# A two-layer encoder on one core: memory and x transposed raw, the norm's weights in the splits, the rows' factor behind the products

## The chip, the cores and the metric

The kernel runs on one core of one Trainium2 chip. The metric is the device time of one execution in microseconds, from the first instruction to the end. The engines are PE (matrix products and transposes), DVE (VectorE), ACT (ScalarE), POOL (GpSimd) and SP, which only issues transfers; ACT and POOL issue some too.

## The reference

Two layers over 512 tokens of width 1024 and 256 memory tokens. All data are float32.

```python
def rmsnorm(x, g):
    y = x * lax.rsqrt(jnp.mean(x * x, axis=-1, keepdims=True) + EPS)
    return y * g

for i in range(2):
    h = rmsnorm(x, norm_g[i])
    mem_h = rmsnorm(mem, mem_norm_g[i])
    proj = h @ w_in[i]                      # mixer heads, memory queries, gate
    o_mix = mixer_dilated(...) if i == 0 else mixer_axial_gqa(...)
    o_mem = memory_attention(q_mem, mem_h, w_mem_kv[i], ...)
    y = concatenate([o_mix, o_mem]) * silu(gate)
    x = x + y @ w_out[i]
```

In both mixers, and in memory attention, each head's queries and keys go through an rmsnorm of their own (128 wide, with the same EPS) before the scores. Layer 0 has 8 heads with three groups of queries, keys and values each; group 0 looks at nearby tokens, groups 1 and 2 at tokens of the same residue mod 4. Layer 1 has 8 query heads on 2 key and value heads.

What matters for the change: a row's norm is a factor r per token times a weight g per feature. A projection of h is r times a projection of g * x, since r belongs to the row and comes out of the sum over features. A head's rmsnorm of r * p with EPS equals the rmsnorm of p with EPS / r**2.

## The kernel before

**Products.** A float32 product is made of three passes over operands split in two: `mm3` multiplies high by high, high by low and low by high, where the high part is the operand rounded to the matrix format and the low part is the remainder. A split is a copy on ACT into the rounded type and a subtraction on DVE (`split`, L156).

**Weights.** `Weights` (L182) streams all weights as pieces of 128x1024, 512 KB each, over SP's queue. `dma` (L229) loads while fewer than `KEEP[...]` pieces are live; `hi` (L278) makes the high part on ACT (L287), `lo` (L292) the remainder on DVE (L297), in a ring of 4. Kinds `T2` and `T2b` are the key and value weights of memory in the layers 0 and 1, eight pieces each. All other projections are products of 2 x 2 blocks with seven block products in place of eight, for which weight pieces are also summed, by DVE (L256) or by adding transfers that POOL issues (`sum`, L243).

**Order.** All engines' instructions are put in order by hand, by one `Driver`. A slot is one step of the weight stream: some 12 products of 128x512 or 24 of 128x256 on PE, then `W.advance()` (splits of weights to come) and `drv.tick()`, which runs every generator that is due: `spawn(gen, delay)` sets one up `delay` slots ahead, `yield n` puts its next step n slots later. `late` and `soon` put a call behind or ahead of a slot's steps.

**Blocks of x.** `s_chunk` (L356) is a projection of x. Its seven products need, in this order, the parts "12", "11", "S1", "S2", "S4", "S3" and "22" of the transposed activation H: blocks of 256 tokens by 512 features and sums or differences of them, each in a high and a low part. Where a part isn't set up yet, the loop ticks on without a product. `evac` results go to `ev` functions that norm, rotate and store.

**The start.** Memory is loaded as two tiles of 128x1024, x as four; the two norm weight rows come as single rows. Eight products with a row of ones (`row_bank`, L585) spread the weight rows over all partitions in PSUM. `norm_1` (L454) makes a row's factor: squares on ACT (one on DVE), and sum, EPS and power -0.5 on POOL (`rstd_of`, L419). `norm_2` (L467) multiplies by the factor and the weights on DVE. `turn4` (L471) transposes four 128x128 blocks on PE, and splits them. Then `mem_kv` (L621) projects memory to keys and values in eight slots; `ahead` (L950), called between its products, norms and transposes the rest of memory. `prep` (L893), spawned in slot `PD`, norms x and makes the parts of H, 128 tokens at a time, with `first_t`, `diffs_t` and `rest_t`. Keys are normed and transposed right after their projection (`ev_k`), values are split (`ev_v`).

**After the start.** The first `s_chunk` is the value projection of group 0, stored to memory as `v0d` and loaded back head by head (`load_v0`, L1104). Then come the memory queries, eight head chunks (`head_chunk`, L1012), each followed by its attention (`attn_a`, L1056) spread over later slots, and three gate chunks m, a and b (`gate`, L749), which apply the gate to attention results loaded from memory. `out_proj` closes the layer; meanwhile `mem_norm(1)` (L595) loads, norms and transposes memory again with the weights of layer 1, and `ev_o` (L1232) norms the new x for the second layer, which goes on in the same way.

## Time and profile before

| | |
|---|---|
| three runs | 967.74, 972.62, 973.62 us; median 972.62 |
| span of the profiled execution | 967.0 us |
| mean granted TensorE clock | 1.000 |
| power steps of row factors and head norms on POOL (L424) | 98, 1059 ns each |
| weight remainders on DVE (L297) | 255, 1237 ns each |
| high parts of weights on ACT (L287) | 255, 1059 ns each |

How to read the profile: times are microseconds unless marked ns. A row of a group has line, engine, operation, written and read tiles, shapes and count, then busy time, mean ns of one, and the idle time of the engine just before with what ended it. A row in time order has start, duration, engine, line, operation, tiles and count, and in brackets the idle time before it. A row of waits has who waited for whom, the total, the number and the longest. A row of stages has the stretch, its length, busy time and count for PE, PEld (weight load), DVE, ACT and POOL, the granted clock, the busy share of the transfer engines and GB/s. L12 is line 12 of the kernel. Matmuls are pipelined and their ends are modelled: the pace of PE is read from start to start.

### The profile page before, as it was taken

How to read it: one execution, taken by the hardware profiler on the slowest of the kernel's cores; microseconds unless marked ns; L12 is line 12 of the kernel's file. 1: busy time of each engine (PE TensorE's matmuls, PEld its weight loads, DVE VectorE, ACT ScalarE, POOL GpSimd, SP SyncE). 2: the span in 40 equal slices, each digit the busy share in tenths (PEclk: the TensorE clock that was granted, in tenths of full speed). 3: DMA queues.
4: the chain of work that ended last, by engine and by line, in shares of the span. 5: the costliest groups of instructions: out<-in, count | busy, mean ns of one | idle time of the engine just before them, and what ended most of it. 6: DMA issues, size and time to landing. Idle time of an engine off the chain costs nothing.

```text
span 967.0 us, 16588 instructions
## 1 busy us (share of the span) xinstructions
PE 946.3 (98%) x5682; PEld 831.4 (86%) x5682; DVE 789.8 (82%) x1411; ACT 682.8 (71%) x1701; POOL 344.3 (36%) x482
## 2 busy tenths in 40 slices
PE   8999999999999999999999999999899999999998
PEld 5879888888888888888899996788899999998786
DVE  5898676888888888888888899779878897769773
ACT  5775689686768686868685657447778887878770
POOL 1513423556554545454726011234333330011011
PEclk9999999999999999999999999999999999999999
DMA  9989956969686868785959889879776686877744
GB/s 357 318 228 344 266 115 170 293 122 268 153 254 141 263 148 257 156 258 132 283 132 252 245 189 305 285 212 362 202 175 137 189 233 168 225 200 177 202 131 131
DMA packets 89129, 209.81 MB, mean 217 GB/s; under 512 B 25298, under 2 KB 36050, under 8 KB 89044
## 3 DMA queue, kind: packets, MB, share of 16 engines
q1 hardware_dynamic: 69892, 145.76, 43.8%
q0 software_dynamic: 17856, 60.83, 33.3%
q10 hardware_dynamic: 1296, 2.16, 0.6%
q8 instruction: 45, 0.74, 0.3%
q14 instruction: 40, 0.33, 0.1%
HBM read 157.27 MB, written 12.65 MB: 176 GB/s over the span
## 4 chain that ended last, share of the span: by engine, by line
PE 80%; DVE 8%; DMA 7%; ACT 3%; issue 1%; SPq 0%; DVEq 0%; ACTq 0%
PE pj L164 21%; PE pj L166 21%; PE pj L165 20%; DVE wo L297 2%; DMA og<-od 2%; PE qT L569 2%; PE ptb L1386 1%; PE sa L1087 1%; PE oo L1189 1%; DMA od<-o 1%; DMA v<-v0d 1%; DMA wl<-in_wall_dram 1%; PE sa L1083 1%; PE pt L1168 1%; PE ob L165 1%
## 5 line engine op out<-in xcount | busy, mean ns | idle before, releaser
L297 DVE TENSOR_TENSOR wo<-wl,wh 128x1024 fp32r<-128x1024 f32 x255 | 314.0, 1237 | 6.2 <-ACT wh L287 6.0
L287 ACT CAST wh<-wl 128x1024 fp32r<-128x1024 f32 x255 | 268.9, 1059 | 53.4 <-PE pj L166 35.5
L164 PE MATMUL pj<-wh,hS 128*128 128x512 f32 (+1 forms) x448 | 163.8, 366 | 0.7 <-ACT sn L364 0.7
L165 PE MATMUL pj<-wo,hS 128*128 128x512 f32 (+1 forms) x448 | 158.2, 353 | 4.3 <-DVE wo L297 4.3
L166 PE MATMUL pj<-wh,hS 128*128 128x512 f32 (+1 forms) x448 | 158.3, 353 | 0.0
L164 PE MATMUL pj<-wh,h 128*128 128x512 f32 (+1 forms) x336 | 122.5, 365 | 0.0
L165 PE MATMUL pj<-wo,h 128*128 128x512 f32 (+1 forms) x336 | 118.5, 353 | 0.1
L166 PE MATMUL pj<-wh,h 128*128 128x512 f32 (+1 forms) x336 | 118.6, 353 | 0.0
L424 POOL TENSOR_TENSOR rstd<-mse,half 128x4 f32<-128x4 f32 (+2 forms) x98 | 103.8, 1059 | 8.2
L165 PEld LDWEIGHTS pj<-wo,hS 128*128 128x128 f32 x448 | 85.0, 190 | 15.4 <-DVE wo L297 5.3
L166 PEld LDWEIGHTS pj<-wh,hS 128*128 128x128 f32 x448 | 84.8, 189 | 12.1
L164 PEld LDWEIGHTS pj<-wh,hS 128*128 128x128 f32 x448 | 84.9, 189 | 11.3 <-ACT sn L364 1.3
L423 POOL TENSOR_SCALAR mse<-hss 128x4 f32<-128x4 f32 (+1 forms) x86 | 46.5, 541 | 126.6 <-ACT junk L557 122.8
L364 ACT COPY sn<-pj 128x512 f32<-128x512 f32 x132 | 73.7, 590 | 19.2 <-PE pj L166 17.9
L557 ACT ACTIVATE junk<-sn 128x128 f32<-128x128 f32 x264 | 79.0, 307 | 1.9 <-DVE sn L375 1.9
L1031 POOL TENSOR_TENSOR ta<-sn,tabs 128x128 f32<-128x128 f32 (+1 forms) x64 | 37.3, 583 | 119.7 <-DVE sn L562 91.5
L381 DVE TENSOR_TENSOR sn<-pj,sn 128x512 f32<-128x512 f32 x99 | 67.6, 685 | 5.6 <-PE pj L166 5.1
L166 PEld LDWEIGHTS pj<-wh,h 128*128 128x128 f32 x336 | 63.6, 189 | 8.9
L165 PEld LDWEIGHTS pj<-wo,h 128*128 128x128 f32 x336 | 63.8, 190 | 8.1 <-DVE wo L297 0.8
L164 PEld LDWEIGHTS pj<-wh,h 128*128 128x128 f32 x336 | 63.7, 190 | 7.2
L271 POOL DMA_DIRECT2D wl<-wl x33 | 29.1, 882 | 113.8 <-DVE wo L297 59.6
L164 PE MATMUL pj<-hS,wh 128*128 128x256 f32 x192 | 56.0, 292 | 0.0
(231 smaller groups left out, 2466.0 us busy)
## 6 DMA issues: line engine op xcount, KB each, us to landing
wl<-in_wall_dram SPq DMA_DIRECT2D x222, 512.0 KB, 6.9
wl<-wl POOLq DMA_DIRECT2D x66, 512.0 KB, 5.9
wl<-in_wall_dram POOLq DMA_DIRECT2D x42, 512.0 KB, 8.6
acc<-sn POOLq DMA_DIRECT2D x16, 256.0 KB, 4.5
od<-o SPq DMA_DIRECT2D x12, 256.0 KB, 5.6
og<-od SPq DMA_DIRECT2D x12, 256.0 KB, 6.1
odb<-o SPq DMA_DIRECT2D x12, 256.0 KB, 3.3
og<-odb SPq DMA_DIRECT2D x12, 256.0 KB, 4.5
```

Of the source, the lines that this page charges most:

```text
L164: T.matmul(o, lh, rh, start=start, stop=False, skip_group_check=True)
L165: T.matmul(o, lh, rl, start=False, stop=False, skip_group_check=True)
L166: T.matmul(o, ll, rh, start=False, stop=stop, skip_group_check=True)
L271: G.dma_start(self.tile[key], self.tile[c, "T2", x], accum_op=ALU.add)
L287: A.copy(wh, self.tile[self.items[i]])
L297: V.tensor_tensor(wo, self.tile[key], wh.bitcast(F32), ALU.subtract)
L364: A.copy(t, b)
L381: V.tensor_tensor(t, b, t, ALU.subtract if q == "12" else ALU.add)
L423: G.tensor_scalar(e, ss, EPS, None, ALU.add)
L424: G.tensor_tensor(r, e, half[:, 0:n], ALU.pow)
L557: A.activation(jk, p[:, j * 128:(j + 1) * 128], AF.Square, scale=QS, accum_out=ss[:, j:j + 1])
L1031: G.tensor_tensor(ta[:, 0:n], xn[:, 0:n, 0:32], ropeA[:, 0, b, s0:s0 + n], ALU.mult)
```

## The change

- Memory and x are no longer normed before they are transposed. The raw rows are transposed. The norm's weights, loaded as 32 rows of 128 and transposed once into a column per block (`gain`), are multiplied in where the operand is split: for x in `gain_hi` (ACT) and `gain_lo` (DVE) and in the sums (`gain_add`), for memory in the split of the key and value weights (`gain_of`, in `hi` and `lo`).
- `prep` makes each part of H for all 256 tokens at once, in its own order; one difference (for "S3") is made on POOL.
- The rows' factors come later: `Rows.square` and `Rows.finish` for memory (`mem_rows`, spawned in slot 9) and x (`x_rows`, slot 11). Keys and values that are projected before memory's factor is there are copied raw to SBUF, and normed or scaled later (`raw`, `kv_raw`).
- Behind the products: head norms get EPS times (mean square + EPS) in place of EPS (`head_sq(..., eps)`); values of groups 1 and 2 are scaled as they are copied; group 0's values are scaled in `scale_v0` on POOL, once a head; gates are multiplied by the factor per token, `rb`, spread over partitions, on POOL (chunks m and a) or DVE (chunk b), with one more slot between. x's factors go through memory to change their layout.
- For layer 1 memory is loaded raw again and only transposed; x of layer 1 is normed as before.
- The row products are gone; two products of a constant tile (512 and 128 columns) stand at the start. Memory, x and the first weight piece are loaded in halves. In the first part of the key projection both token blocks use the first weight piece before the second.
- `chunk` takes all its PSUM banks at its start; constants: `PD` 2 to 3, `KEEP_1` 9 (was 10) for the first blocked chunk.

```diff
         def hi(self, force=False):
...
-            A.copy(wh, self.tile[self.items[i]])
+            g = self.gain_of(i)
+            if g is None:
+                A.copy(wh, self.tile[self.items[i]])
+            else:
+                for k in range(2):
+                    cs = slice(k * 512, (k + 1) * 512)
+                    A.activation(wh[:, cs], self.tile[self.items[i]][:, cs], AF.Copy, scale=g[:, k:k + 1])
...
-            V.tensor_tensor(wo, self.tile[key], wh.bitcast(F32), ALU.subtract)
+            g = self.gain_of(i)
...
+                    V.scalar_tensor_tensor(wo[:, cs], self.tile[key][:, cs], g[:, k:k + 1], wh[:, cs].bitcast(F32), ALU.mult, ALU.subtract)
...
+    def gain_hi(hi, src, g, ks=range(4)):
+        for k in ks:
+            A.activation(hi[:, k], src[:, k], AF.Copy, scale=g[:, k:k + 1])
+
+    def gain_lo(lo, src, g, hi, ks=range(4)):
+        for k in ks:
+            V.scalar_tensor_tensor(lo[:, k], src[:, k], g[:, k:k + 1], hi[:, k].bitcast(F32), ALU.mult, ALU.subtract)
+
+    def gain_add(dst, src, g, other):
+        for k in range(4):
+            V.scalar_tensor_tensor(dst[:, k], src[:, k], g[:, k:k + 1], other[:, k], ALU.mult, ALU.add)
...
     def prep():
...
+        turned(0)
+        yield 1
+        turned(1)
+        yield 1
+        yield from scaled("12", xr[0, 1], gx[1])
+        turned(2)
+        yield 1
+        yield from scaled("11", xr[0, 0], gx[0])
+        turned(3)
+        yield 1
+        u = m4(name="xu").rearrange("p (k t) -> p k t", k=4)
+        for k in range(4):
+            A.activation(u[:, k], xr[1, 1][:, k], AF.Copy, scale=gneg[:, 4 + k:5 + k])
+        yield 1
+        gain_add(u, xr[1, 0], gx[0], u)
+        G.tensor_tensor(xr[1, 0], xr[0, 0], xr[1, 0], ALU.subtract)
+        yield 1
+        yield from plain("S1", u)
+        yield 1
+        gain_add(xr[0, 0], xr[0, 0], gneg[:, 0:4], u)
+        yield 1
+        yield from plain("S2", xr[0, 0])
+        yield 1
+        gain_add(xr[0, 1], xr[0, 1], gx[1], xr[0, 0])
+        yield 1
+        yield from plain("S4", xr[0, 1])
+        yield 1
+        yield from scaled("S3", xr[1, 0], gx[0])
+        yield 1
+        yield from scaled("22", xr[1, 1], gx[1])
...
+    mem_tiles()
+    mem_load(0, 0)
+    W.dma(1, True)
+    mem_load(1, 0)
+    W.dma(1)
+    mem_load(0, 1)
+    mem_load(1, 1)
+    W.dma(2)
+    for c in range(4):
+        x_load(c)
         W.dma(1)
...
+    for n in (512, 128):
+        T.matmul(at("idle")[:, 0:n], idle[:, 0:128], idle[:, 0:n], start=True, stop=True)
...
+    mem_turn(M, mem_nat, 0, 0)
     W.hi(True)
+    W.lo()
+    mem_turn(M, mem_nat, 1, 0)
     W.hi(True)
     W.lo()
...
+        def scale_v0():
+            G.tensor_tensor(v0, v0, r0s[:, :, None].to_broadcast([128, 4, 128]), ALU.mult)
...
         scale(1)
         yield Y[6]
+        scale_v0()
         scale(0)
         turn(1)
...
+                if rb is not None:
+                    tv = t.rearrange("p (h t) -> p h t", h=2)
+                    (V if g == 2 else G).tensor_tensor(tv, tv, rb[:, None, ts].to_broadcast([128, 2, 256]), ALU.mult)
+                    yield 1
                 th = s2(name="th")
                 A.activation(th, t, AF.Tanh, scale=0.5)
```

`scaled(k, ...)` is `gain_hi`, one slot, `gain_lo`, and the part is set up; `plain(k, ...)` the same with a plain copy and subtraction. `turned(c)` transposes 128 tokens of x and copies them to SBUF on ACT.

More of the change, by code (lines that the diff above doesn't have):

```diff
@@ L331, in trunk_kernel, with chunk @@
     W = Weights()
-    def chunk(units, nb, group, evac, pre=None):
-        ps = [None] * nb
+    def chunk(units, nb, group, evac):
+        ps = [pj() for _ in range(nb)]
         for u in range(units):
@@ L551, in rest_t, with head_sq @@
         yield 1
-    def head_sq(p, n=4):
+    def head_sq(p, n=4, eps=None):
         ss = sm(n, "hss")
@@ L881, in trunk_kernel @@
         W.dma(1)
-    W.dma(2)
-    tabA = s2(name="tabA")[:, 0:256].rearrange("p (b c d) -> p b c d", b=2, c=4)
-    grA = s2(name="grA")[:, 0:192].rearrange("p (s c) -> p s c", s=6)
     nc.sync.dma_start(gc, gcol)
-    for c in range(4):
-        nc.sync.dma_start(xt[c], xv[c])
-        if c % 2:
-            W.dma(2)
     H, H2 = {}, {}
-    xb = [halves(t) for t in xt]
-    def prep():
-        n = {}
-        for c in range(5):
-            if c < 4:
-                n[c] = norm_1(xb[c])
-            if c:
-                norm_2(xb[c - 1], n[c - 1], rows["x"])
-            if 1 < c < 4:
-                first_t(H, xb[c - 2], c - 2)
-            yield 1
-        for c in range(2):
-            yield from diffs_t(H, xb[2 + c], c)
-            drv.spawn(rest_t(H, c, (2, 2, 2)), 1)
-            yield 1
+    gx = [gain[:, 4 * j:4 * j + 4] for j in range(2)]
@@ L972, in ev_v0 @@
         yield 1
-    km, vm = mem_kv(0, M, ahead)
+    km, vm = mem_kv(0, M, between)
     s_chunk(512, H, ev_v0)
@@ L990, in ev_qm @@
         i, j = int(q[0]) - 1, int(q[1]) - 1
-        r = head_sq(t)
+        r = head_sq(t, 4, RX.eps[:, 2 * i:2 * i + 2])
         yield 1
```

276 lines of the change are left out of this document (175 added, 101 removed).

## The prediction

> **What bounds the kernel now.** I read the page first, then the busy time of each engine by stage, then who kept PE waiting, and last the first microseconds in order of time, because most of the edit lies there. From the page:
>
> ```profile
> span 967.0 us, 16588 instructions
> ...
> PE 946.3 (98%) x5682; PEld 831.4 (86%) x5682; DVE 789.8 (82%) x1411; ACT 682.8 (71%) x1701; POOL 344.3 (36%) x482
> ```
>
> PE is busy nearly all the time, and the edit takes no product away: what can be won is time in which PE stands still, in all 967.0 - 946.3 = 20.7 us, plus time that it spends on work that is not a product. Busy time by stage (PE, PEld, DVE, ACT, POOL):
>
> ```profile
> 0.00:30.00 30.00, 26.74 (x90) 17.47 (x91) 15.84 (x22) 19.49 (x43) 8.42 (x19) 1.00 0.94 369
> 30.00:80.00 50.00, 48.42 (x225) 38.86 (x224) 48.74 (x61) 34.89 (x60) 17.16 (x18) 1.00 0.91 257
> ...
> 200.00:500.00 300.00, 300.00 (x1578) 254.59 (x1577) 251.93 (x572) 219.51 (x660) 161.48 (x242) 1.00 0.75 199
> 500.00:545.00 45.00, 45.00 (x377) 44.89 (x376) 37.10 (x81) 27.54 (x71) 18.29 (x27) 1.00 0.87 244
> 560.00:600.00 40.00, 38.16 (x222) 32.34 (x221) 39.15 (x67) 26.52 (x40) 6.07 (x7) 1.00 1.00 252
> 600.00:640.00 40.00, 37.59 (x187) 30.94 (x186) 29.77 (x40) 20.47 (x34) 9.07 (x12) 1.00 0.86 267
> ```
>
> The reader is to see two stretches in which DVE, not PE, has no room: 30 to 80 us (48.74 of 50) and 560 to 600 us (39.15 of 40). In the head stage, 200 to 500 us, DVE has 48 us of room and PE none. PE's own waits, first for 0 to 100 us, then for 560 to 700 us:
>
> ```profile
> PE pj L165 <- DVE wo L297: 1.5, 2, 0.9
> PE pj L164 <- ACT act L158: 0.9, 2, 0.7
> ```
>
> ```profile
> PE pj L165 <- DVE wo L297: 4.2, 3, 2.9
> ```
>
> **The change part by part.** First the start, which stands in time order:
>
> ```profile
> 0.73 0.35 SPq L874 DMA_DIRECT2D row<-in_mem_norm_g_dram  x1
> 1.42 0.37 SPq L880 DMA_DIRECT2D m<-in_mem_dram  x1
> 1.83 0.43 SPq L238 DMA_DIRECT2D wl<-in_wall_dram  x1
> 2.35 7.16 PE L590 MATMUL row<-row,tabs 1*128 1x512 f32 x8 [2.35 <-DMA row<-in_mem_norm_g_dram]
> 5.37 0.63 ACT L462 ACTIVATE sq<-m 128x512 f32<-128x512 f32 x1 [3.15 <-DMA m<-in_mem_dram]
> 6.61 1.04 ACT L287 CAST wh<-wl 128x1024 fp32r<-128x1024 f32 x1 [0.52 <-DMA wl<-in_wall_dram]
> 7.42 0.75 DVE L469 SCALAR_TENSOR_TENSOR m<-m,rstd,row 128x512 f32<-128x512 f32 x1 [1.36 <-POOL rstd L424]
> 9.44 1.11 PE L475 MATMUL xT<-ident,m 128*128 128x128 f32 x4
> 10.59 0.58 ACT L158 CAST act<-xT 128x512 fp32r<-128x512 f32 x1 [1.36 <-PE xT L475]
> 11.23 0.79 PE L164 MATMUL pj<-wh,act 128*128 128x512 f32 x1
> ```
>
> *Start.* Today the first product runs at 11.23. Ahead of it stand the loads, the squares (5.37), the root on POOL, the scaling on DVE (7.42), and on PE the eight row products that spread the norm weights (2.35 to 9.51); only then come the transposes at 9.44. The change takes squares, root, scaling and row products off this path. What is left: load, transpose, cast, split of weights. A memory tile of 512 KB takes 5.37 - 1.42 = 3.95 us from issue; the weight tile issued 0.41 us behind it is there at 6.61, 1.24 us later, so 512 KB cost about 1.2 us of transfer and 256 KB about 0.6. Estimate: the first half tile, issued at 0.73, is there at 0.73 + 3.95 - 0.6 = 4.1; two half weight tiles at 4.7 and 5.3; the next half memory tile at 5.9. Transposes to 4.1 + 1.11 = 5.2, the cast to 5.8. Four more transposes are queued on PE ahead of the first product, 5.9 to 7.0; beside them ACT splits the first weight half (half of 1.04, so 6.4) and DVE its remainder. First product at 7.0: **-4.2 us**. Bounds: were a half tile as slow as a whole one, 7.6 (-3.6); were the second set of transposes hidden, 6.4 (-4.8). The transposition of the gain rows waits for two small loads on ACT's queue; the nearest row, the 4 KB row issued at 0.73 and used at 2.35, took 1.6 us, which is earlier than the half tile, so I cost it at nothing; if it came last it would cost its lateness one to one. On SP's queue x is now eight half loads and not four, four more issues of about 0.4 us, behind the first four weight tiles and three slots ahead of their use: 0. The stores and loads that carry the rows' factors through memory, and the load of rb, stand on SP behind slot 15 and are used much later: 0.
>
> *Clock.* Steps between products in the chain that ended last:
>
> ```profile
> 14.58 0.43 PE pj L165
> 15.01 0.28 PE pj L166
> 15.29 0.23 PE pj L164
> ```
>
> PE runs at half pace until 15.0, 3.8 us after the first product, although the row products had kept it busy since 2.35. The same 3.8 us behind 7.0 lose the same; 0. The Trainium skill, "TensorE: Matmul & The Clock Gate", Part 1, says that the clock opens after about 3.4 us of sustained activity in windows that do not start with the kernel; by that rule the two full-height idle products might open it earlier. The trace agrees with the half pace, not with the row products counting as activity. At most 9 products at 0.20 us less each, -1.8, are at stake, and as much the other way if gaps in the early products keep it shut.
>
> *Waits behind the start.* The transposes of the second half of memory move six products later, so ACT's casts have time: of the 0.9 us on L158 I take **-0.9** (0 to -0.9). From 30 to 80 us PE can only stay ahead if DVE has less to do. Prices on DVE:
>
> ```profile
> L256 DVE TENSOR_TENSOR wl<-wl 128x1024 f32<-128x1024 f32 x5 | 6.1, 1221 | 0.0
> L469 DVE SCALAR_TENSOR_TENSOR x<-x,rstd,row 128x512 f32<-128x512 f32 x8 | 5.6, 749 | 1.0 <-POOL rstd L424 1.0
> ...
> L469 DVE SCALAR_TENSOR_TENSOR m<-m,rstd,row 128x512 f32<-128x512 f32 x4 | 2.9, 742 | 1.4 <-POOL rstd L424 1.4
> ...
> L618 DVE SCALAR_TENSOR_TENSOR kmT<-qT,gc,kmT 128x512 fp32r<-128x512 f32 x2 | 1.5, 748 | 0.0
> ...
> L543 DVE TENSOR_TENSOR f<-f,f 128x512 f32<-128x512 f32 x2 | 1.4, 692 | 0.1
> ```
>
> ```profile
> 548.59 0.42 DVE L1093 CUSTOM_DVE_ANT_0 p<-sa,tabs 128x256 f32<-128x256 f32 x1
> ```
>
> Removed: norm_2 of x and memory, 5.6 + 2.9; one square, 0.7; and of first_t, diffs_t and rest_t 22 operations of 128x512 (4 + 2 + 8 remainders, 8 sums) at 0.69, 15.2. Together 24.4 us. Added: 16 gain_lo and 12 gain_add operations of 128x256; no such row exists, the nearest two-input one of that size is 0.42, the bounds are half of 0.748 (0.37) and 0.55; 28 x 0.42 = 11.8. Three plain remainders at 1.22, 3.7. Eight memory weight tiles split in two halves, 8 x (2 x 0.748 - 1.22) = 2.2. Together 17.7. One S3 difference goes to POOL (below, 1.9 of delay). Net 24.4 - 17.7 - 1.9 = 4.8 us less for DVE before 80 us: enough to follow a PE that is 5 us ahead, with nothing to spare. Keys and values are also put off (their head_sq, scaling and splits leave the early slots and come back after slot 19), six operations of 0.69 to 0.75, which moves 4 us of DVE out of the tight part into its end. So the 1.5 us that PE waits for wo go: **-1.5** (bounds -1.5 and +3: S1, S2 and S4 are now set in the very slot that uses them, two to five slots later than before, and if ACT or DVE is late there, PE waits for a whole split of 1.2 us, two or three times).
>
> *Factors behind the products, heads and gates.* New are 8 scale_v0 and 8 gate products (chunks m and a) on POOL, 128x512 each, and 4 gate products on DVE (chunk b). The eps addition changes its form on POOL, four elements either way, 0. The largest POOL product of today and DVE beside it:
>
> ```profile
> 74.40 4.63 POOL L923 TENSOR_TENSOR tabs<-tabA,grA 128x768 f32<-128x768 f32 x2 [1.06 <-DVE grA L920]
> ```
>
> ```profile
> 62.98 2.35 DVE L297 TENSOR_TENSOR wo<-wl,wh 128x1024 fp32r<-128x1024 f32 x2
> ...
> 74.83 5.29 DVE L297 TENSOR_TENSOR wo<-wl,wh 128x1024 fp32r<-128x1024 f32 x2
> ```
>
> The reader is to see that while POOL multiplied for 4.63 us, two remainders on DVE took 5.29 instead of 2.35: 2.9 us lost, 0.63 us per us of POOL. This speaks against the change. At 4.63/2 x 512/768 = 1.55 us a product, 16 of them are 25 us of POOL and up to 16 x 0.97 = 15.5 us of DVE; the S3 difference, twice as long, costs the 1.9 us above. The Trainium skill, "GPSIMD Engine Reference", section 1, gives the cause: POOL's way to SBUF is shared with DVE instructions that have two SBUF inputs. This trace agrees (5.29 against 2.35). Its section 3.1 has 4497 ns for 2048 elements, by which 512 would be an estimated 1.1 us and the DVE loss 11 us in place of 15.5. In the head stage DVE has 48 us of room in 300, so of about 1 us a head little reaches PE: **+0.5** (0 to +15.5). scale_v0 also stands in POOL's line ahead of root products and weight sums, but its load is issued five steps earlier, so it should not block; ACT's cast of v0 comes one step later. Were the cover gone, each head would lose up to 1.55 us.
>
> In chunk b, 560 to 600 us, DVE is full, and 4 x 0.69 = 2.8 us are added where it already makes PE wait (the 4.2 us above): **+1.4**, half of it, since DVE has 10 us of room again right after (29.77 of 40) (bounds 0 and 2.8).
>
> *Layer two.* Four scalings and squares of memory go (4 x 0.74 on DVE), eight weight tiles split dearer (+2.2 on DVE). They nearly cancel; **0** (bounds -2 and +1).
>
> Sum: -4.2 - 0.9 - 1.5 + 0.5 + 1.4 = -4.7 us, a span of 962.3. The three runs have a median of 972.62 and a lowest of 967.74; the span of 967.0 lies 5.6 below the median, and I carry this over: 962.3 + 5.6 = 967.9, said as **968**.
>
> **The rivals.** *The shared port decides (slower).* If the head stage's slots are so tight that DVE's delay reaches PE one to one, the 15.5 us and the 2.8 us are paid in full: -6.6 + 15.5 + 2.8 = +11.7, 984. For it: the 5.29 row, and chunks m and a bring POOL products close together. Against it: PE at 300.00 of 300 with DVE at 84%. It turns the sign once 4 us of the 15.5 reach PE beside the 2.8; it passes 1% from about 14.
>
> *The start isn't kept.* DVE at 48.74 of 50 sets the pace; if my price of 0.42 is 0.55, its saving falls from 4.8 to 1.2 us and the just-in-time parts make PE wait. Then all but about 1 us is given back, and with the later +1.9 the time is 973 to 974. For it: the slots counted above. Against it: the deferred keys and values.
>
> *More falls away.* The first product comes at 6.4 (-4.8), the clock opens before it (-1.8), both DVE waits go as DVE is freed (-0.9 - 1.5), the second layer's relief counts (-2), and chunk b hides its additions: -11.0, 962. For it: each is a bound of a row above. Against it: all must come together.
>
> **How the numbers follow.** The forecast, 964 to 971, has 0.37; more falling away 0.30; the start not kept 0.18; the shared port 0.15. One per cent, about what a measurement of this kernel can tell from no change, is 962.9 and 982.3. Faster by over 1%: the part of "more" at or below 962.9 and the forecast's lower tail, 0.30. Slower by over 1%: the port case with the worst of the start not kept, 0.18. Within: 0.52. Range 958 to 980: it takes in the larger gain with the unknown clock, the start not kept, and leaves out the port case's upper part. Both signs do not share most of the chance; the likeliest one's own range is 964 to 971.
>
> **What would show it.** Right: first product near 7, a half pace of some 4 us behind it; the first product of chunk "12" some 5 us earlier than now; DVE clearly under 48 of 50 in 30 to 80 us; wo durations over 2 us only beside scale_v0. Wrong: first product after 8.5; PE waits on S1, S2 or S4 remainders of over 2 us; PE waits for wo in the head stage, which has none of weight today; a 560 to 600 stretch with PE under 36.

## The result, and the profile after

The changed kernel is slower: 985.9 us median (984.96 to 987.4, 4 runs) against 970.75 us (967.74 to 973.62, 4 runs), a ratio of 1.0176 with an interval of 1.0154 to 1.0198. The prediction was 968 us, in a range of 958 to 980, with 0.18 for slower by over 1%. The page of the profiled execution (984.96 us), with PE's busy time and the granted clock in 40 slices:

```profile
span 983.2 us, 16655 instructions
...
PE 947.0 (96%) x5677; PEld 835.0 (85%) x5677; DVE 794.9 (81%) x1424; ACT 693.2 (71%) x1724; POOL 355.6 (36%) x484
...
PEclk9979999999999999999999999999999999999999
```

PE's busy time is what it was (947.0 for 946.3), though not of the same parts: the row products' 7.2 us are gone, and the products into `pj` took 5.6 us more. The 16 us are time in which PE stands still. The same stages as before:

```profile
0.00:30.00 30.00, 25.91 (x109) 19.82 (x110) 14.14 (x24) 19.36 (x33) 0.19 (x4) 1.00 0.95 352
30.00:80.00 50.00, 42.20 (x183) 33.75 (x181) 37.27 (x53) 38.19 (x82) 19.86 (x22) 0.90 0.86 234
80.00:130.00 50.00, 47.08 (x291) 41.85 (x290) 38.04 (x46) 29.71 (x70) 15.52 (x18) 0.97 0.98 292
...
200.00:500.00 300.00, 300.00 (x1559) 254.17 (x1558) 251.77 (x576) 222.76 (x666) 171.08 (x256) 1.00 0.79 202
500.00:545.00 45.00, 40.99 (x336) 40.24 (x335) 37.65 (x67) 28.62 (x74) 25.63 (x32) 0.99 0.84 221
```

From 30 to 80 us PE lost 6 us (42.20 for 48.42) although DVE, the suspected bound, was busy for 37.27 us in place of 48.74 (part of this is work held up by the same wait: experiment 3, without it, has 44.98); from 500 to 545 us PE lost 4 (40.99 for 45.00). Through the heads, 200 to 500 us, it lost nothing.

Stages shift against each other when one kernel runs ahead, so the exact place is read from the starts of the same product in both kernels. The table was worked out from the traces: start of the n-th product into `pj` in the kernel before, and how much later the others start it (minus is earlier). "Both" and "all three" are the experiments 3 and 12 below, "no factor" is experiment 5.

```
product  before    after   both  all three  no factor  what lies there
      0    11.2    -2.94  -2.94    -3.19      -2.93    first product
     24    21.5    -4.95  -4.18    -4.25      -4.75    key projection of memory, second half
    144    54.5    -6.33  -5.52    -5.60      -6.09    part S1 of the first projection of x
    216    73.1    +2.30  -4.21    -3.69      -4.64    behind parts S2 and S4
    440   106.4    +4.03  -3.34    -2.18      -3.76    first head chunk begins (432)
    480   116.3    +8.20  -1.39    -1.34      -1.15    its part S1, behind the memory queries' transposes
   1152   315.4    +8.03  -1.59    -1.51      -1.34    heads
   1992   529.4    +7.67  -1.98    -1.89      -1.73    chunk a, part S1; m's gates are being applied
   2088   544.6   +13.77  +4.14    +1.05      -1.23    chunk a, part 22
   2256   570.4   +14.83  +5.20    +0.47      -1.88    chunk b, part 22; a's gates are done
   2480   631.5   +14.54  +4.79    +0.26      -4.81    output product
   2640   673.1   +13.67  +3.93    -0.59      -5.66    layer two begins
   2688   678.9   +15.85  +6.10    +1.56      -3.51
   4079   962.7   +16.02  +6.06    +0.81      -3.47    last
```

From the lead of 6.3 us at product 144 to the end 22.4 us are lost, and three places hold 18.9 of them: 8.6 us at part S2 (products 144 to 216), 4.2 us ahead of product 480 (5.9 from 216 on), and 6.1 us from 1992 to 2088, where PE is at gate chunk a while the other engines finish the gates of chunk m: this stretch is called m's gates below. The rest comes in steps of 1 to 2 us. The heads give 0.5 us back. The granted clock fell to half at 56.1 us for 10.2 us, and for 3.4 us at 117.6, 544.2 and 697.8, each time within a wait of PE or up to 1 us behind one; before it stayed full from 15.0 us to the end. PE's waits after, for 0 to 100 us, 100 to 130 us and 500 to 560 us (who waited for whom, total, times, longest):

```profile
PE pj L165 <- ACT hS L993: 7.2, 1, 7.2
PE gT L1082 <- DMA grow<-in_mem_norm_g_dram: 1.5, 1, 1.5
...
PE qT L1133 <- DVE sn L620: 2.4, 1, 2.4
...
PE pj L165 <- DVE sn L397: 4.0, 1, 4.0
```

**First place: a buffer that is not free.** The split of part S2 (L993) stands on ACT behind the squares of x (L514). In time order, from the trace of the changed kernel:

```profile
45.91 1.06 ACT L993 CAST hS<-xu 128x1024 fp32r<-128x1024 f32 x1
...
49.04 0.33 SPq L1107 DMA_DIRECT2D v0d<-sn  x1
...
53.44 0.39 PE L167 MATMUL pj<-wh,hS 128*128 128x512 f32 x1
...
54.52 0.63 ACT L514 ACTIVATE sq<-x 128x512 f32<-128x512 f32 x1 [7.55 <-DMA v0d<-sn]
...
59.96 1.04 ACT L993 CAST hS<-xT 128x1024 fp32r<-128x1024 f32 x1
...
61.05 0.80 PE L165 MATMUL pj<-wh,hS 128*128 128x512 f32 x1 [7.22 <-ACT hS L993]
```

The bracket in the fourth row is what is to be read: ACT idled 7.55 us until a *store* had left. The square writes its 128x512 results, which nobody reads, into a fresh tile of the pool `s2`; the buffer it was given still held a block of group 0's values on its way to memory. The raw rows of x, eight tiles, and four raw tiles of keys and values now lie in that pool of fourteen. All of ACT's work behind the square waited too, among it three splits of weights that stand ahead of S2's, and PE with it. Of the 8.6 us lost here, 7.2 are this wait; the products behind it ran at half pace up to 66.3 us.

**Second place: 4-byte packets in the way of the weights.** SP's own waits from 55 to 100 us, and the transfers from 72 to 97 us (GB/s in 40 slices of 0.625 us; packets; then what was issued, count, KB each, median us from issue to landing), after:

```profile
SPq L1051 <- POOL rx L522: 11.3, 1, 11.3
...
SPq L1056 <- DMA rblk<-rx: 3.7, 1, 3.7
```

```profile
GB/s 33 0 0 0 0 4 3 13 66 26 13 79 59 26 59 33 20 52 20 26 7 26 210 420 416 393 262 249 236 236 275 239 259 229 292 262 315 290 388 403
DMA packets 2405, 3.71 MB, mean 148 GB/s; under 512 B 1367, under 2 KB 1367, under 8 KB 2403
...
wl<-in_wall_dram SPq DMA_DIRECT2D x5, 512.0 KB, 12.2
...
rx<-rnat SPq DMA_DIRECT2D x2, 0.2 KB, 14.2
...
rblk<-rx SPq DMA_DIRECT2D x1, 2.0 KB, 11.1
```

and the same view and window of the kernel before:

```profile
GB/s 419 419 361 282 242 262 269 243 282 236 262 256 220 331 429 429 413 380 295 236 233 220 318 364 420 403 400 344 347 370 413 416 416 423 419 419 419 419 419 419
DMA packets 2810, 8.67 MB, mean 347 GB/s; under 512 B 314, under 2 KB 314, under 8 KB 2808
...
wl<-in_wall_dram SPq DMA_DIRECT2D x12, 512.0 KB, 7.9
```

The store of x's row factors stands on SP one slot behind their computation, and SP waited 11.3 us for it with weight loads queued behind. Then the store `rblk`, 2 KB in 512 packets of 4 bytes, took 11.1 us to land (74.7 to 85.8). Until it had landed all transfers together moved 3 to 79 GB/s, although three weight pieces and two blocks of values were issued meanwhile; from then on it was 210 and more. In the three experiments that leave the store here (1, 4 and 8) it takes as long, with 33 to 37 GB/s moved meanwhile and 290 to 307 in the 5 us behind it; in the nine that have it later it takes 8.8 to 15.5 us, with 146 to 185 GB/s and then 204 to 383. The loads of the factors (0.2 and 1.5 KB, 14.2 and 17.0 us) are not of this kind: their packets started only at 94 to 97 us, and up to 412 GB/s moved beside them. Why the store takes so long isn't shown. In 25 us five weight pieces were issued in place of twelve, and 3.71 MB moved in place of 8.67. The Trainium skill, "DMA: Bandwidth & Descriptors", section "Rules for kernel authors", says that a transfer whose last dimension is not contiguous becomes one descriptor per element; the trace agrees, with 1367 packets under 512 B for 314. The late weights reach PE by way of POOL, whose adding transfers stand ahead of the queries' row factor:

```profile
113.64 0.85 POOL L274 DMA_DIRECT2D wl<-wl  x1 [7.32 <-issue]
114.20 0.52 POOL L443 TENSOR_TENSOR mse<-hss,rx 128x4 f32<-128x4 f32 x1
114.80 1.03 POOL L445 TENSOR_TENSOR rstd<-mse,half 128x4 f32<-128x4 f32 x1
```

**Third place: GpSimd's gate products beside VectorE's two-input steps.** The changed kernel at m's gates (L835), beside steps of the last two heads:

```profile
532.22 1.57 POOL L835 TENSOR_TENSOR sn<-sn,rb 128x512 f32<-128x512 f32 x1
532.27 2.60 DVE L313 TENSOR_TENSOR wo<-wl,wh 128x1024 fp32r<-128x1024 f32 x1
...
537.00 1.96 DVE L1271 TENSOR_TENSOR d<-nmM,stp 128x8 f32<-128x8 f32 x1
...
537.35 1.58 POOL L835 TENSOR_TENSOR sn<-sn,rb 128x512 f32<-128x512 f32 x1
...
539.07 0.21 ACT L1274 ACTIVATE e<-d 128x16 f32<-128x16 f32 x1 [4.62 <-DVE d L1272]
...
540.93 2.12 POOL L835 TENSOR_TENSOR sn<-sn,rb 128x512 f32<-128x512 f32 x1 [2.00 <-DVE sn L397]
...
540.70 1.22 DVE L313 TENSOR_TENSOR wo<-wl,wh 128x1024 fp32r<-128x1024 f32 x1
541.83 1.76 DVE L840 SCALAR_TENSOR_TENSOR sn<-th,sn 128x512 f32<-128x512 f32 x1
...
543.79 0.68 DVE L397 TENSOR_TENSOR sn<-pj,sn 128x512 f32<-128x512 f32 x1
```

and the difference of eight numbers and the gate's step behind the tanh in the kernel before:

```profile
526.28 0.68 DVE L768 SCALAR_TENSOR_TENSOR sn<-th,sn 128x512 f32<-128x512 f32 x1
...
527.67 0.17 DVE L1132 TENSOR_TENSOR d<-nmM,stp 128x8 f32<-128x8 f32 x1
```

Each of the three GpSimd products holds up one VectorE step with two inputs: 2.60 us for a remainder that takes 1.22 at 540.70, 1.96 for a difference of eight numbers a row that took 0.17 before, 1.76 for a step of 0.68. That is 1.4 + 1.8 + 1.1 = 4.3 us in one chain, and at its end stands L397, which empties the bank that PE needs: PE's wait of 4.0 us. The other 2 of the 6.1 us lie behind this wait, where the clock is at half pace until 547.6 us.

### The profile page after: what moved, and what is told of

It is laid out like the page before. It is cut to its first block, busy times and chain, and to the rows that moved or that the text cites. A ratio compares the mean times of both kernels' runs of the same rounds, so it can differ in the third digit from the quotient of the medians.

```text
span 983.2 us, 16655 instructions
## 1 busy us (share of the span) xinstructions
PE 947.0 (96%) x5677; PEld 835.0 (85%) x5677; DVE 794.9 (81%) x1424; ACT 693.2 (71%) x1724; POOL 355.6 (36%) x484
## 4 chain that ended last, share of the span: by engine, by line
PE 69%; DVE 14%; DMA 7%; ACT 4%; issue 3%; POOL 2%; SPq 0%; DVEq 0%; POOLq 0%; ACTq 0%
PE pj L167 18%; PE pj L165 18%; PE pj L166 18%; DVE wo L313 4%; DMA wl<-in_wall_dram 2%; PE qT L627 2%; PE ptb L1529 1%; DMA wl<-wl 1%; PE sa L1223 1%; PE sa L1219 1%; PE pt L1307 1%; PE oo L1328 1%; DVE sn L397 1%; DVE wo L317 1%; DMA og<-odb 1%
## 5 line engine op out<-in xcount | busy, mean ns | idle before, releaser
L313 DVE TENSOR_TENSOR wo<-wl,wh 128x1024 fp32r<-128x1024 f32 x239 | 294.5, 1236 | 14.7 <-ACT wh L297 14.5
L297 ACT CAST wh<-wl 128x1024 fp32r<-128x1024 f32 x239 | 252.7, 1059 | 47.2 <-PE pj L167 27.4
L445 POOL TENSOR_TENSOR rstd<-mse,half 128x4 f32<-128x4 f32 (+2 forms) x90 | 100.0, 1111 | 7.1
L165 PEld LDWEIGHTS pj<-wh,hS 128*128 128x128 f32 x448 | 86.0, 192 | 17.5 <-ACT hS L993 7.6
L167 PEld LDWEIGHTS pj<-wh,hS 128*128 128x128 f32 x448 | 85.9, 192 | 14.0 <-DVE hS L995 1.7
L166 PEld LDWEIGHTS pj<-wo,hS 128*128 128x128 f32 x448 | 86.2, 193 | 12.4 <-DVE wo L313 2.1
L397 DVE TENSOR_TENSOR sn<-pj,sn 128x512 f32<-128x512 f32 x99 | 67.6, 684 | 1.4 <-PE pj L167 1.1
L274 POOL DMA_DIRECT2D wl<-wl x33 | 28.9, 877 | 109.4 <-DVE wo L313 55.3
L264 POOL DMA_DIRECT2D wl<-wl x33 | 31.0, 968 | 85.3 <-DMA wl<-in_wall_dram 44.3
```

Source lines behind the costliest of these rows:

```text
L165: T.matmul(o, lh, rh, start=start, stop=False, skip_group_check=True)
L166: T.matmul(o, lh, rl, start=False, stop=False, skip_group_check=True)
L167: T.matmul(o, ll, rh, start=False, stop=stop, skip_group_check=True)
L264: G.dma_start(self.tile[key], self.tile[c, "T1", x], accum_op=ALU.add)
L274: G.dma_start(self.tile[key], self.tile[c, "T2", x], accum_op=ALU.add)
L297: A.copy(wh, self.tile[self.items[i]])
```

## The experiments

Ratios are to the kernel before on the same chip, with the 95% interval. They are told by mechanism; the numbers are the order in which they ran.

**1 and 2: the square's buffer, and the place of the stores.** Experiment 1 writes the squares over their own rows, which nobody reads later; experiment 2 puts the stores of the row factors five slots further behind.

```
-                A.activation(s2(name="sq"), t[j], AF.Square, ...
+                A.activation(t[j], t[j], AF.Square, ...
```

```
         RX.finish()
-        yield 1
+        yield 6
         nc.sync.dma_start(r_nat.rearrange("(p b) -> p b", b=4), RX.r)
```

> The squares of x and memory are written over their own rows instead of a fresh scratch buffer. Theory W (waits): ACT stood 7.6 us because the scratch buffer of a square was still being read by the first store of v0; PE's wait of 7.2 us on the S2 part falls under 1 us, the half pace of 10.2 us behind it goes, and the time falls by 8 to 10 us to about 977. Rival J (parts just in time): S1, S2 and S4 are set up too late anyway, PE still waits over 4 us there, and the time falls by less than 3 us.

> The two stores of x's row factors are issued five slots later; nothing else. Theory W: SP stood 11.3 us on these stores with weight loads behind them, which made the adding transfers and with them POOL's root at 114 us late; that wait (2.4 us) and its half pace (3.4 us) go, the time falls by 3 to 5 us to about 982. Rival: the weights are late only because of the wait at 53 us; then the wait at 114 us stays and the time moves by less than 1 us.

Experiment 1: 978.64 us, ratio 1.0096 (1.0062 to 1.0131), 0.8% less than the change as it stands. Its waits of PE from 0 to 100 us have no L993 on ACT left:

```profile
PE gT L1082 <- DMA grow<-in_mem_norm_g_dram: 2.5, 1, 2.5
PE pj L167 <- DVE hS L995: 2.3, 3, 1.5
```

Product 216 now starts 3.44 us earlier than before, not 2.30 later, and the half pace at 56 us is gone. The other two places are untouched (at product 480 it is +0.86, with PE waiting 2.6 us for the queries; m's gates cost the same 6.1). This settles the first place. What now shows there is the row of L995: PE waits 2.3 us for remainders of x's parts on DVE, the lateness that the prediction had bounded at 3.

Experiment 2: 984.69 us, 1.0157 (1.0127 to 1.0188): the total can't be told from the change's, and the 3 to 5 us expected aren't there. Alone it brings little: the wait at S2 is still there, and longer in this profile (product 216 at +5.87); but from there to product 480 it loses 3.5 us where the change as it stands loses 5.9, and PE's wait for the queries is 1.5 us for 2.4.

**3: both.**

> Both edits together. Theory W: 12 to 14 us less, about 973, with PE waiting under 1 us in the first 130 us. Rival (both waits have one cause): no more than the better one of the two alone.

975.87 us, 1.0068 (1.0043 to 1.0094), 0.3% below experiment 1, with intervals that overlap, as those of experiment 2 and the change do. Product 480 is 2.2 us earlier than in experiment 1, but 0.8 us of that stands at the first product already. So the totals don't settle the second cure, and the 12 to 14 us expected of both were 10. The profiles show it: from product 216 to 480 the four kernels with the stores at their old place (the change and experiments 1, 4 and 8) lose 4.3 to 8.1 us, the six with the stores five slots later (2, 3, 5, 6, 7 and 12) 2.4 to 3.7. PE still waits 2.6 us for remainders of x's parts and 1.8 us for the queries. From 70 to 95 us its transfers (same view) moved nearly twice as much as the changed kernel's:

```profile
DMA packets 3540, 6.82 MB, mean 273 GB/s; under 512 B 1497, under 2 KB 1497, under 8 KB 3538
...
rblk<-rx SPq DMA_DIRECT2D x1, 2.0 KB, 9.1
```

The small packets are no fewer; SP no longer waits 11.3 us ahead of them, and the weights are already under way. Up to product 1992 this kernel is 2 us ahead of the one before. What is left stands at m's gates, 6.1 us.

**9: the stores still later.** As experiment 3, with `yield 30`.

> Squares over their own rows as before, and the row-factor stores and loads 29 steps later instead of 5, some 80 us, so that they stand past the weights of the first two stages. Theory Q (the 4-byte packets of these stores and loads take the weights' place on the transfer engines, so the adding transfers and with them the row factor of the queries are late at 110 us): against the third kernel the wait of TensorE at 107 falls from 1.8 us to under 0.5, product 480 starts 1 to 2 us earlier (from -1.4 to -2.5 to -3.5 against before), the rest is kept, median 973.5 to 975. Rival (the weights' stream as such is the bound there, since the start is 4 us earlier): product 480 stays at -1.0 to -1.8, median 975.5 to 976.5.

976.43 us, 1.0085 (1.0066 to 1.0103): not better than experiment 3. The wait at 107 us fell from 1.8 to 1.5, product 480 came to -2.02, between what the two theories gave, and the time is the rival's. But the 4-byte packets now land in the first heads, at 169 to 190 us, and make a new wait there:

```profile
PE sa L1219 <- DVE qk L1183: 1.9, 1, 1.9
```

```profile
rblk<-rx SPq DMA_DIRECT2D x1, 2.0 KB, 13.8
```

and SP, with weight loads to issue, waits until that store has landed:

```profile
SPq L241 <- DMA rblk<-rx: 7.2, 1, 7.2
```

From product 576 to 744 its lead goes from -2.03 to +0.14: put there, these transfers cost 2.2 us at a place where nothing else was changed (in experiments 10 and 11, which have them there too, 4.8), so they do hold up weights. At the old place most of the wait at 107 us is left without them, so most of what experiment 3 still loses there isn't theirs; the stream of weights, which the earlier start does not make faster, is a reason that was not tried.

**5: no factor in the gates.** As experiment 3, without the row factor in the gates.

```
-            if c == "m":
-                rb = s2(name="rb")
-                nc.sync.dma_start(rb, r_blk.rearrange(...)...)
+            rb = None
```

> This kernel is the third one (squares over their own rows, row-factor stores five steps later; 975.87 us) with x's row factor left out of the gates: no broadcast row is loaded, no product is made and the tanh waits for one step less, so the gates lack that factor. Theory G (GpSimd's products, through the port that both use and through the one step more, make the reader of the bank late at 540 us): the wait of TensorE at 540 falls from 5.0 us in all to under 1, the half-pace stretch at 535.6 goes, product 2328 starts 5 to 7 us earlier against before than in the third kernel (+5.2 becomes -2 to 0), median 969 to 971. Rival P (the products merely lie there, and the wait comes from the last head's longer chain of value scaling on GpSimd): the wait stays over 3 us, median 974 to 976.

965.71 us, 0.997 (0.9955 to 0.9986), 10 us less than experiment 3 and better than the 969 to 971 expected. The stretch of m's gates (product 1992 to 2088) now costs 0.5 us against before, in place of 6.1, and what lies behind gives time back, 3.6 us up to product 2480 where experiment 3 lost 0.7. Its longest wait of PE for L397 from 500 to 700 us:

```profile
PE pj L165 <- DVE sn L397: 1.7, 2, 1.3
```

So applying one number per token to twelve gate tiles, with the load of `rb` and the slot more, costs 9.5 us (-3.47 for +6.06 at the last product), more than the change wins without it. It is also the only one of these kernels that is faster than the one before.

**4, 10 and 11: the same products on VectorE.** Experiment 4 puts all twelve on VectorE in the kernel as changed, experiment 10 in experiment 9's, and experiment 11 leaves those of chunk a on GpSimd.

```
-                    (V if g == 2 else G).tensor_tensor(tv, tv, rb[...
+                    V.tensor_tensor(tv, tv, rb[...
```

> The eight gate products of the chunks m and a are made on DVE instead of POOL. Theory P (shared port and POOL's line): the PE wait of 4 us at 540 us and its half pace go, 4 to 6 us less, about 980, although DVE gets 5.5 us more work. Rival S (the extra step): the wait comes from the step put ahead of the gate's tanh, not from the engine; then the wait stays within 1 us of 4 and the time within 2 us.

> The kernel before it (rows 29 steps later, squares over their own rows), with all twelve products of the gates on VectorE, none on GpSimd. Theory G (at 540 us the price is the time in which VectorE stands still beside GpSimd's products, 1.6 to 2.1 us each, more than 0.68 us for the same product on VectorE): the wait at 540 falls from 5.0 us to 1 to 2.5, product 2256 comes 3 to 6 us earlier than with GpSimd's products, median 968 to 971, near the time before. Rival V (VectorE is the bound in this stage, and each product on it, 0.68 us, is paid in full): 4 to 5 us for the gates as with GpSimd, median 973 to 975.

> As the kernel with all gate products on VectorE, but the four of the second gate chunk (about 555 to 580 us, behind the last head) on GpSimd again; those of the first and the third on VectorE. If what counts is that the last head's short two-input steps are no longer held up, the gain at 540 us is kept and the time is within 1 us of the kernel with all on VectorE, 968 to 971. If GpSimd's products cost as much in the second chunk, it is 1 to 2 us slower than that, and the difference stands between products 2088 and 2328.

Experiment 4: 983.58 us, 1.0146 (1.0114 to 1.0178), a total that can't be told from the change's, with a longer loss at S2 in its profile; m's gates cost 4.0 us (product 1992 to 2088) in place of 6.1, and PE's longest wait for L397 is 2.3 us in place of 4.0, so neither of its two theories is met in full. Experiment 10: 973.06, 1.0047 (1.0029 to 1.0065) against 1.0085 of experiment 9, which is the clean comparison: 0.4% less, m's gates 2.8 us in place of 6.1. Its total lies in the rival's range, 973 to 975; but from product 1992 to 2256 it loses 2.2 us where experiment 9 loses 7.2, which the rival would not have, and its early lead was smaller (product 216 at -3.1 for -4.6) and the wait in the first heads larger (3.0 us). Experiment 11: 975.82, 1.0075 (1.0055 to 1.0095): with chunk a's products back on GpSimd it starts product 2256 1.8 us later than experiment 10, and 1.6 of this arises from product 2088 on. Three of these four products lie there, at 550 to 564 us; the differences of eight numbers a row lie at 531 and 588. So in this profile GpSimd's product is dear beside other work of a full VectorE too, not only beside the heads' short steps. In all experiment 11 is 2.8 us slower, a little more than was expected for this case, with intervals that overlap.

**6: no factor on group 0's values.** As experiment 3, without `scale_v0`.

> This kernel is the third one (975.87 us) with the scaling of the first group's values on GpSimd left out, eight products in the heads, so those values lack the row factor. The rival of the prediction (the shared port decides: the splits beside these products run longer and TensorE waits) would have 1 to 2 us a head back: median 962 to 968. Theory N (nothing in the heads is near its limit: the drift of the after kernel over the eight heads is -0.5 us): products 1152 to 1920 stand within 0.5 us of the third kernel's, median 975 to 976.

974.22 us, 1.0067 (1.0047 to 1.0086), against 1.0068: no difference. Products 1152 to 1920 start within 0.5 us of experiment 3's. Of the eight GpSimd products six lie in the heads, at 244 to 490 us in experiment 3, one at 537 and one at 599. The six cost nothing that can be measured; VectorE has 46 us of 300 to spare there.

**7: plain splits of layer two's key and value weights.** As experiment 3; the kernel leaves out that norm's weights.

> This kernel is the third one (975.87 us) in which the splits of the second layer's key and value weights go back to one copy and one subtraction each, without that norm's weights, which are then left out of that layer's memory keys and values. Theory T (the weights' two half-width steps with a scale are dearer on ScalarE and VectorE, and between 690 and 697 us TensorE waits for such a split): the +2.2 us of that stage goes, median 973 to 974.5, product 3960 starts 1.5 to 2.5 us earlier than in the third kernel. Rival (the wait there comes from the row factor's chain in the keys, not from the weights): median 975.5 to 976.5.

973.84 us, 1.0042 (1.0018 to 1.0066). The median falls where the theory put it, but its interval overlaps experiment 3's, and in its profile product 3960 starts only 0.5 us earlier and not 1.5 to 2.5. The stage itself tells more. From product 2480 to 2688 the change and the eleven other experiments all lose 1.3 us against before (1.29 to 1.32), and this one wins 0.4: 1.7 us, as the theory had it. PE's wait for L620 there is 0.4 us in place of 1.6; a wait of 1.9 us for a remainder stays, and the kernel before has one of 2.9. That product 3960 doesn't show it comes from elsewhere: this profile was 0.9 us behind experiment 3's at product 2480, and the clock fell at 883.3 us for 3.4.

**8: PE kept busy through its wait.** In the kernel as changed, products without a reader ahead of part S2.

```
+            if act is H and a == "S2" and not filled:
+                filled.append(1)
+                o = at("fill")[:, 0:256]
+                for _ in range(48):
+                    T.matmul(o, H["11"][:, 0, 0, 0:128], H["11"][:, 0, 0], start=True, stop=True)
```

> This kernel is the after kernel (985.9 us) with 48 products of 128x256 without a reader put into TensorE's queue just ahead of the group that waits for the second difference's split at 53 us, some 5 us of work, so that TensorE waits less at one piece; nothing else changes. Theory C (a wait of TensorE of some 3 us or more is followed by a stretch at half pace, 10.2 us at 56.1 here, which costs about as much again as the wait): the half-pace stretch at 56 shrinks to 3.4 us or goes, product 360 comes 2 to 5 us earlier, median 981 to 984. Rival D (the weights' splits and VectorE bound these 30 us anyhow, so that full pace there only ends in another wait): product 360 within 1 us, median 985 to 987. Rival E (the added work is only added): median 988 to 991.

985.33 us, 1.0175 (1.0147 to 1.0203): no gain in the total, though the half pace at 56 us is gone altogether. The stage 50 to 70 us, first of the changed kernel and then of this one:

```profile
50.00:70.00 20.00, 12.35 (x43) 8.99 (x41) 11.64 (x16) 12.58 (x24) 4.99 (x9) 0.74 0.83 230
```

```profile
50.00:70.00 20.00, 16.08 (x91) 13.80 (x92) 11.93 (x17) 11.28 (x21) 3.74 (x8) 1.00 0.67 171
```

At full clock (1.00 for 0.74) the products behind S2 wait for remainders on VectorE, in all 3.3 us, which at half pace they hardly did (0.4):

```profile
PE pj L167 <- DVE hS L1000: 3.3, 3, 2.0
```

Product 360 starts 1.4 us later than in the changed kernel (+5.38 for +4.03), but the two profiles don't start alike: the store held ACT for 10.03 us in this one, for 7.55 in the other, so the first product of S2 came 3.0 us later (64.08 for 61.05), and not by the added products, which ended at 62.3. From that product to product 216 this kernel takes 12.93 us. The changed kernel and experiments 2 and 4, which have the half pace, take 14.26 to 14.72, experiments 1 and 3, which don't have the wait, 12.3 to 12.4. So by the profiles the half pace behind S2 cost some 1.4 us: what theory C names is there, but smaller. The total doesn't show it, and lies in theory D's range; its interval is 2.7 us to either side. The short stretches at 117.6, 544.2 and 697.8 us were not tried.

**12: all three cures.** Squares over their own rows, stores five slots later, gate products on VectorE.

> All three cures that held so far at once: squares over their own rows, the row-factor stores 5 steps later (not 29), all gate products on VectorE. If the three prices add up, the stage from product 1992 to the end loses 3 us against before, as with the gates on VectorE and the rows 29 steps later, but starts it 2 us ahead, as the third kernel does: product 1992 at -1.5 to -2.5, the end at +0.5 to +1.5, median 969 to 971, within 0.3% of before. If the lead is eaten again (what the earlier start brings is taken by the next stage that is short of slack), 972 to 974, as with the rows 29 steps later.

971.22 us, 1.0036 (1.0023 to 1.0049), product 1992 at -1.9 and the last at +0.8: where the sum of the three prices had put them, the time a little above (969 to 971, within 0.3%). Four fifths of the loss is undone, and the change still wins nothing. PE's wait at m's gates, and the step of eight numbers a row:

```profile
PE pj L165 <- DVE sn L397: 1.8, 1, 1.8
```

```profile
526.39 0.17 DVE L1271 TENSOR_TENSOR d<-nmM,stp 128x8 f32<-128x8 f32 x1
```

In the chain ahead of this wait 1.1 us are again a VectorE step beside a GpSimd product: a gate product that takes 0.68 elsewhere, beside the seventh of the products on group 0's values:

```profile
529.91 1.36 POOL L1250 TENSOR_TENSOR v<-v,rx 128x512 f32<-128x512 f32 x1
...
530.03 1.80 DVE L835 TENSOR_TENSOR sn<-sn,rb 128x512 f32<-128x512 f32 x1
```

The sum by ratios, in per cent of the time before: 1.76 for the change; 0.80 go with the square's buffer, 0.28 more with the stores and 0.32 more with the gate products on VectorE (both between runs whose intervals overlap; experiments 9 and 10, whose intervals don't meet, give 0.38 for the last); 0.36 are left. Without the gate factor it would be -0.30, so the factor on VectorE, 0.66, turns what is left.

## Why the prediction was wrong, point by point

- **Start, -4.2.** The mechanism was right and the size off. The first product came at 8.29, not 7.0: the transposes began at 5.70, not 4.1, since PE's queue held the transposition of the gain rows in front. The half tile had landed at 3.60, the gain rows, issued at 1.32 and 1.79, only at 5.35. In time order:

```profile
5.48 0.28 PE L1082 MATMUL gT<-ident,grow 32*128 32x32 f32 x1 [1.51 <-DMA grow<-in_mem_norm_g_dram]
...
5.70 1.11 PE L493 MATMUL xT<-ident,m 128*128 128x128 f32 x4
...
8.29 0.77 PE L165 MATMUL pj<-wh,act 128*128 128x512 f32 x1
```

  The prediction costed them at nothing by a row load of 1.6 us, and named the price if they came last. The lead was there later all the same: -4.95 at product 24, -6.33 at product 144.
- **Clock, 0.** Right at the start: half pace for 3.5 us behind the first product. That PE would stand still long enough for the clock to fall again later was not foreseen; by experiment 8 it cost some 1.4 us behind S2, and for the other three stretches the cost is open.
- **Waits behind the start, -0.9 and -1.5, by VectorE's relief of 4.8 us.** VectorE was relieved (44.98 for 48.74 from 30 to 80 us in experiment 3), and where nothing else stood in the way PE kept its lead (experiment 3: -4.18 at product 24, -4.21 at 216). The price of a `gain_lo` or `gain_add` was a little low: 28 took 13.4 us and not 11.8, 0.48 each. The bound of +3 named the right instructions, the splits of S1, S2 and S4 set just in time: with the buffer's wait gone, PE waits 2.3 to 3.3 us for their remainders (experiments 1, 3 and 12). What failed is that the sum counted engines and left out buffers: x's raw rows and the raw keys and values moved into a pool of fourteen tiles, and a square that needs a scratch tile waited for a store. In place of -1.5 there were 7.2 us of waiting at this one place.
- **Row-factor stores and loads on SP, "used much later: 0".** This step failed. When a transfer's result is used doesn't matter to what is queued behind its issue: SP waited 11.3 us for the factors, and then little else moved for 11.1 us, while a store in packets of 4 bytes was on its way. From product 216 to 480 moving the stores is worth 1.5 to 2.4 us by the profiles (2.8 lost in experiment 3 for 4.3 in experiment 1, 3.5 in experiment 2 for 5.9 in the change); by the totals 0.2 to 0.3%, within the uncertainty.
- **Heads, +0.5 (0 to +15.5).** Right in the heads: -0.5, and experiment 6 shows no difference. The price of a product was too high there, 1.55 us where the eight on v0 have a median of 1.09 us. The estimate of 1.1 us worked out from the Trainium skill, "GPSIMD Engine Reference", section 3.1, agrees with this.
- **Gates.** This is the step that decided. The eight products of chunks m and a were put in with the heads' and with the room of the heads (252 of 300 us), and only chunk b was priced by its own stage. But chunk m's four lie at 523 to 543 us, where the last two heads, the gates and the splits share VectorE, and chunk a's at 545 to 572, up to the stretch that the prediction itself had called full. In place of at most 1.9 us (+0.5 and +1.4) the gate factor cost 9.5.
- **Layer two, 0.** A little outside its bounds (-2 and +1): 0.9 us are won from product 2480 to 2640 and 2.2 lost by 2688 (+14.54, +13.67, +15.85), a net of +1.3. The dearer splits cost 1.7 there (experiment 7); without them 0.4 would be won.
- **The rivals.** "The shared port decides" had the mechanism that mattered, and placed it in the heads, where it is free. It was given 0.15, and its time of 984 comes near the result, but from another sum, which is luck: of 17 us, the port's part beyond VectorE's own work is 3. "The start isn't kept" (0.18) named the place where the lead went, but VectorE as the cause; it was a buffer.
- **The 5.6 us carried over** from the profiled execution to the median were too many: in the later comparisons the kernel before has medians of 967.5 to 969.4 us.

## What to carry to other kernels

Give every instruction that is moved ahead of a tight stage its full list: the engine, the queue that issues it, and the buffer that it writes, even when nobody reads what it writes. Price an added operation in the stage in which it runs, not by the mean room of its kind; one multiplication by a per-token factor is cheap on a partition axis, where a copy carries it along, and dear on the free axis, where it is an instruction of its own. If a factor must pass through memory to change its layout, count its packets and not its bytes.

## What the runs showed of the hardware that was not expected

- A VectorE step of 128x8 with two inputs took 1.96 us in place of 0.17 beside a GpSimd product that ended just as it did: here the small step waited for the whole product. The Trainium skill, "GPSIMD Engine Reference", section 1, says that GpSimd's way to SBUF is shared with VectorE instructions with two SBUF inputs, and the trace agrees. Which of the two goes first isn't settled: the remainder at 540.70, recorded 0.23 us ahead of a GpSimd product, took its usual 1.22, and the product 2.12, where the eight of them have a median of 1.59; but the step of eight numbers is recorded 0.35 us ahead of its product too, and waited.
- The granted clock fell to half behind waits as short as 2.4 us (at 117.6) and, in experiment 10, behind two of 1.5 and 1.9 us (at 687.5), each time for 3.4 us; all such stretches lasted 3.4, 6.8 or 10.2 us. The length of a wait alone doesn't decide: in experiments 3, 5 and 12 the same two waits, and in the kernel before one of 2.85 us (at 679.2), were followed by no fall.
- A store of 2 KB in 512 packets of 4 bytes took 8.8 to 15.5 us to land, and while it was on its way all transfers together moved 33 to 37 GB/s in four of these kernels, 146 to 185 in the nine others. Loads in packets of 4 bytes didn't have this effect (up to 412 GB/s beside them in the changed kernel), though they took 14.2 us to land behind weights, longer than the 512 KB pieces, 12.2.
